# The attention half of a joint projection, placed in the second instead of the third input pass

## The chip, the cores and the metric

The kernel runs on one core of one Trainium2 chip. The metric is the device time of one execution, in microseconds; the time before is the median of three runs, 2733.04 us (2730.65 to 2734.66). The profile is of a further execution of the same program.

## The reference

One encoder layer on 2048 tokens of width 1024, in float32: a wide input projection, chunked band attention (8 heads) beside an mLSTM (4 heads), each projected back to the width and gated, an output projection, a squared-ReLU feed-forward layer and a last norm.

```python
xn = rms_norm(x, mix_norm_g)
aq, ak, av, mq, mk, mv, mo, ipre, fpre, ga, gm = jnp.split(xn @ w_in, points, axis=-1)
att = chunk_band_attention(heads(aq), heads(ak), heads(av), rel_bias)
mqk = jax.nn.silu(causal_depthwise_conv(jnp.concatenate([mq, mk], -1), conv_w, conv_b))
hm = mlstm_chunkwise(*heads(mqk), heads(mv), ipre + b_igate, fpre + b_fgate)
mlstm_out = jax.nn.sigmoid(mo) * head_rms_norm(hm, mh_norm_g)
y = jax.nn.sigmoid(ga) * (att @ w_att_proj) + jax.nn.sigmoid(gm) * (mlstm_out @ w_mlstm_proj)
x = x + y @ w_out
x = x + jnp.square(jax.nn.relu(rms_norm(x, ffn_norm_g) @ w_up)) @ w_down
return rms_norm(x, final_norm_g)
```

The two products in the line of `y` are what the change moves, for the first half of the tokens.

## The kernel before

**Blocks and products.** The tokens are four blocks of 512; blocks 0 and 1 make the first half, blocks 2 and 3 the second. Each float32 product is made of three matmuls of rounded parts (the operand is cast, and the remainder subtracted: one ScalarE and one VectorE instruction, called a split, lines 1348 and 1353 for activations, 582 and 584 for weights). The large products use a seven-product scheme: the operand matrix is cut in four quarters, from which sums are made (lines 1973 to 2015), seven products are formed, and their results are combined in `combine` (copies on ScalarE, line 2033, additions on VectorE, line 2041).

**The input projection of the second half** is written in three passes over its ten column groups, called names here, in the order `gm0, gm1, q, mq, vm, ga0, k, mk, ga1, mo` (`IN_ORDER`). Of the seven products, pass 1 makes those of `BATCHES[0]` (0, 3, 1), pass 2 those of `BATCHES[1]` (2, 4) and pass 3 those of `BATCHES[2]` (5, 6). A name takes 48 matmuls in pass 2 and in pass 3 (line 743), `vm` 96 (line 748). Between the passes, partial sums are parked in HBM (`park`), and up to six are loaded ahead. In passes 1 and 2 the names go one at a time; pass 3 takes them in pairs (`PAIRS`). The code numbers the passes g = 0, 1, 2, and a place in them (g, i).

**The operands of the passes** lie in `r` tiles, of which there are 28 in all (`rpool`). Sixteen of them form a ring for the passes: 12 for pass 1 and 4 of pass 2, and when pass 1 lets its 12 go, 4 more go to pass 2 and 8 to pass 3. Those eight are loaded from `xu` at the start of pass 2 (`take_batch`, `take_u1`, line 2346).

**The joint projection** of blocks 0 and 1 (`joint`) has two halves: half 0 is attention's product with `w_att_proj`, half 1 is the mLSTM's with `w_mlstm_proj`. Each half makes seven products for each of two column groups: 168 matmuls, at line 1134. Its operands are loaded from `mix`, where attention and mLSTM have stored their outputs (`take_joint`, line 1092): in two groups, one after the other, each with five `ctx` tiles (of 16) and four loads, and 14 `r` tiles in all. A half loads its 16 gate tiles through `temp` tiles (line 1167). Half 0 leaves its gated products in the four `sc` tiles and six `r` tiles, and half 1 adds to them (lines 1190 and 1205) and stores the sum `yp`, which the output projection loads.

Before the change, when pass 3 begins, the eight ring tiles that pass 2 has let go come back to `rpool`, the four `sc` and six `r` tiles are taken, and both halves' operands are asked for. Half 0 stands ahead of the third name of pass 3 (`q`), half 1 ahead of the fifth (`vm`). Ahead of `q`, eight more matmuls (line 1663) of the gate columns are made.

**What orders the work.** The kernel's steps are threads; a planner in the program steps them in a clock of its own, with a cost for each instruction, and writes each engine's instructions in the order in which they came. Where several are ready at once, the one goes first whose due time, computed back from a first pass of the planner, is the earliest. The order on each engine and on SP's DMA queue is then fixed; on the chip each instruction waits for its semaphores, and what is behind it waits with it. The dense products are one thread, in the order of the loops of `in_far`.

Of the kernel before, what the change touches and what calls it, by code (L numbers as in the profile page):

```python
# [52 lines left out]
BATCHES = ((0, 3, 1), (2, 4), (5, 6))  # L53
# [6 lines left out]
SUMS.update({at: N_Q - N_F + n for n, at in enumerate(((1, 1), (1, 6), *((4, i) for i in range(6))))})  # L60
SUMS.update({(0, 4): N_Q + 9, (0, 6): N_Q + 10})
J_ORDER = (0, 2, 3, 4, 5, 1, 6)
JOINT = {(2, 2): 0, (2, 4): 1}
PROJ = {2: (4, 0), 3: (6, 1)}

ORDER = (0, 1, 3, 2, 5, 4, 6)
# [241 lines left out]
def off(name):  # L308
    return 3 if name in ("mq", "mk") else 0
# [3 lines left out]
class Layer:  # L313
# [101 lines left out]
    def weights(self):  # L415
# [9 lines left out]
        for g, batch in enumerate(BATCHES):  # L425
            for pair in PAIRS if g == 2 else [(i,) for i in range(len(IN_ORDER))]:
                i = pair[0]
                if (g, i) in JOINT:
                    yield from (("half", (JOINT[g, i], t)) for t in range(7))
                vm = g == 0 and IN_ORDER[i] == "vm"  # L430
# [323 lines left out]
    def in_far(self, A, aev, ring):  # L754


        fl = self.fl
        E4 = lambda: [Event() for _ in range(NT)]
        pair = lambda of: [[of(), of()] for _ in IN_ORDER]
        kept = pair(E4)  # L760
        self.banks.want = 4
        for g, batch in enumerate(BATCHES):
            if g > 0:
                got, gev, room = ahead
            if g == 1:
                fl.spawn(self.take_batch(BATCHES[2], A, aev, ring), 1)
            if g == 2:
                fl.put(self.rpool, *(yield "get", ring, 8))
                J = [self.operands() for _ in range(2)]
                slots = (yield "get", self.sc, 4), (yield "get", self.rpool, 6), [[Event(), Event()] for _ in range(6)]  # L770
                fl.spawn(self.take_joint(0, J), 1)
            if g == 2:
                for pair in PAIRS:
                    if (g, pair[0]) in JOINT:
                        yield from self.joint(0, JOINT[g, pair[0]], J, slots)
                        if JOINT[g, pair[0]] == 1:
                            fl.put(room, *[0] * 4)
                    yield from self.in_last(pair, batch, A, aev, ring, got, gev, room)
                break
            for i, name in enumerate(IN_ORDER):  # L780
                self.sum_at(g + 1, i)
                if g < 2 and i == len(IN_ORDER) - 1:
                    ahead = pair(lambda: [None] * NT), pair(E4), Pool([0] * 6)
                    fl.spawn(self.unpark(g + 1, kept, *ahead), 1)
                if (g, i) in JOINT:
                    yield from self.joint(0, JOINT[g, i], J, slots)
                    if JOINT[g, i] == 1:
                        fl.put(room, *[0] * 4)
                tok = name == "vm"
                finish, o = (self.after_vm(), 0) if tok else (self.after_in(1, name), off(name))  # L790
                release = ring if i == len(IN_ORDER) - 1 else None
                bank, clear, every = [], E4(), range(NT if tok else 2)
                yield from self.product(tok, batch[0], A, aev, bank, None, release)
                if g == 0:
                    t, tev, other = [None] * NT, E4(), []
                    for n in every:
                        fl.spawn(self.park_first(n, t, tev[n], bank[n], clear[n], o), 1)
                    for m in batch[1:] if not tok else batch[:0:-1]:
                        if m == 3:
                            yield from self.product(tok, m, A, aev, other, None, release)  # L800
                            for n in every:
                                fl.spawn(self.park_u2(i, n, t, tev[n], other[n], kept[i][0][n], o), 1)
                        else:
                            yield from self.product(tok, m, A, aev, bank, clear, release)
                            for n in every:
                                fl.spawn(self.finish_ps(finish, n, bank[n]), 1)
                    if i == 1:
                        (bk,) = yield "get", self.banks, 1
                        yield from self.gate_mm(bk, A, ((0, 0), (1, 4)), True, True)
                        fl.spawn(self.gates(2, bk), 1)  # L810
                    continue
                for n in every:
                    fl.spawn(self.park_v(i, n, got[i], gev[i], bank[n], clear[n], kept[i][1][n], o) if g == 1 else
                             self.finish_far(finish, n, "a22", 1, got[i], gev[i], bank[n], clear[n], o, room), 1)
                yield from self.product(tok, batch[1], A, aev, bank, clear, release)
                for n in every:
                    fl.spawn(self.finish_far(finish, n, "a12" if g == 1 else "a21", 0, got[i], gev[i], bank[n], None,
                                             o, room), 1)
                if i == 1:
                    (bk,) = yield "get", self.banks, 1  # L820
                    yield from self.gate_mm(bk, A, ((2, 0),) if g == 1 else ((6, 8),), True, True)
                    fl.spawn(self.gates_kept(bk) if g == 1 else self.gates(3, bk, True), 1)
        self.banks.want = 0
        fl.put(self.rpool, *(yield "get", ring, 8))
# [241 lines left out]
    def project(self, b, room):  # L1066
# [14 lines left out]
        if b % 2 == 1:  # L1081
            O = self.y_operands = self.operands()
            for k in range(4):
                fl.spawn(self.take_y(b // 2, k, *O), 2)
    def take_joint(self, s, J):

        def row(x):
            def load(b, j, a):
                i = 4 * x + (j if j < 4 else j - 2)
                yield "wait", [self.blk[2 * s + b]["mix_ev"][i]]  # L1090
                yield "sp", 800, 2000
                self.nc.sync.dma_start(a, self.mixd.ap()[2 * s + b, i])

            return load

        for x in range(2):
            for k in range(2):
                yield from self.take_parts(row(x), 1.0, k, self.splitter(k, *J[x], 1.0), J[x][1], pool=self.ctx)

    def joint(self, s, x, J, slots):  # L1100

# [1714 lines left out]
```

## Time and profile before

| | |
|---|---|
| median of three runs | 2733.04 us |
| profiled execution | 2726.03 us |
| its span, first to last instruction | 2724.2 us |
| TensorE busy | 2706.6 us, 99% |
| VectorE busy | 2109.8 us, 77% |
| ScalarE busy | 1543.0 us, 57% |
| GpSimd busy | 48.4 us, 2% |
| mean granted clock of TensorE | 0.999 |
| moved by DMA | 683.01 MB, 251 GB/s |

Times in the profile are microseconds from the span's start. PE is TensorE's matmuls, PEld its weight loads, which run beside them; DVE is VectorE, ACT is ScalarE, POOL is GpSimd, and SPq is the queue in which SyncE issues DMAs. `L1134` is line 1134 of the kernel. A row of the timeline has the start, the length, the engine, the line, the operation with what it writes and reads, the count of instructions, and in brackets the idle time of the engine before it with what ended it. Matmuls overlap, so a row's length over its count is the time that one of them costs. In a row of DMA issues stand the count, the size of each and the median time from the issue to the landing.

The second pass's `ga0`, `k`, `mk`, `ga1`, `mo` are made from 832 to 887, the third pass from 887 to 1089; the output projection (line 712) follows.

### The profile page before, as it was taken

What the parts mean: (1) busy time and instruction counts of PE and PEld (TensorE: products, weight loads), DVE (VectorE), ACT (ScalarE), POOL (GpSimd) and SP (SyncE); (2) the same over time, 40 slices, a digit from 0 to 9 for tenths busy, and PEclk for the clock granted to TensorE, in tenths of its full rate; (3) what the DMA queues carried; (4) which work ended last, traced back from release to release, by engine and by line L of the source; (5) the groups of instructions that cost most, each with busy time, mean ns of one, the idle gap of its engine ahead of it and who ended that gap; (6) DMA issues with size and microseconds to landing.
All of it is one profiled execution on the core that took longest, in us unless ns stands there. A gap on an engine that the chain in (4) does not pass through costs nothing.

```text
span 2724.2 us, 38141 instructions
## 1 busy us (share of the span) xinstructions
PE 2706.6 (99%) x12784; PEld 2253.2 (83%) x12784; DVE 2109.8 (77%) x3750; ACT 1543.0 (57%) x2685; POOL 48.4 (2%) x79
## 2 busy tenths in 40 slices
PE   9999999999999999999999999999999999999998
PEld 8878888888888888888888888888888888888887
DVE  7878876888876899887768888889798665657675
ACT  6555456776753545566556766656345565554443
POOL 0000000000000000000000000000000000000000
PEclk9999999999999999999999999999999999999999
DMA  8777889878768889867768787766864454578863
GB/s 309 276 261 278 292 288 308 264 239 276 265 231 282 292 306 323 278 215 263 267 235 285 246 261 223 238 232 219 277 229 160 163 197 159 189 271 281 275 241 134
DMA packets 339304, 683.01 MB, mean 251 GB/s; under 512 B 37684, under 2 KB 66996, under 8 KB 339108
## 3 DMA queue, kind: packets, MB, share of 16 engines
q1 hardware_dynamic: 338388, 679.52, 73.2%
q8 instruction: 100, 1.64, 0.3%
q10 hardware_dynamic: 720, 1.06, 0.1%
q14 instruction: 96, 0.79, 0.1%
HBM read 461.41 MB, written 215.88 MB: 249 GB/s over the span
## 4 chain that ended last, share of the span: by engine, by line
PE 91%; DVE 3%; DMA 2%; issue 2%; ACT 1%; SPq 0%; POOL 0%; ACTq 0%; POOLq 0%; DVEq 0%
PE bank L712 40%; PE bank L743 9%; PE bank L644 8%; PE bank L645 8%; PE bank L643 8%; PE bank L1134 3%; PE bank L748 2%; PE bank L1612 2%; PE bank L1580 2%; PE bank L1505 2%; PE bank L970 1%; DVE wsp L584 1%; PE bank L1855 0%; PE bank L1840 0%; DMA ctx<-park 0%
## 5 line engine op out<-in xcount | busy, mean ns | idle before, releaser
L712 PE MATMUL bank<-r,wsp 128*128 128x512 f32 x4872 | 1110.3, 389 | 0.8 <-DVE wsp L584 0.7
L712 PEld LDWEIGHTS bank<-r,wsp 128*128 128x128 f32 x4872 | 913.2, 188 | 192.4 <-DVE wsp L584 1.2
L582 ACT CAST wsp<-wraw 128x1024 fp32r<-128x1024 f32 x437 | 459.1, 1051 | 495.3 <-PE bank L712 165.0
L584 DVE TENSOR_TENSOR wsp<-wraw,wsp 128x1024 fp32r<-128x1024 f32 x437 | 533.7, 1221 | 233.6 <-ACT wsp L582 228.6
L643 PE MATMUL bank<-r,wsp 128*128 128x512 f32 x960 | 379.3, 395 | 0.0
L645 PE MATMUL bank<-r,wsp 128*128 128x512 f32 x960 | 375.2, 391 | 0.0
L644 PE MATMUL bank<-r,wsp 128*128 128x512 f32 x960 | 375.2, 391 | 0.0
L743 PE MATMUL bank<-r,wsp 128*128 128x512 f32 x1512 | 368.1, 393 | 1.2 <-DVE ctx L894 1.0
L743 PEld LDWEIGHTS bank<-r,wsp 128*128 128x128 f32 x1512 | 279.0, 188 | 56.8 <-issue 1.0
L645 PEld LDWEIGHTS bank<-r,wsp 128*128 128x128 f32 x960 | 180.3, 188 | 38.4
L644 PEld LDWEIGHTS bank<-r,wsp 128*128 128x128 f32 x960 | 180.5, 188 | 33.6
L643 PEld LDWEIGHTS bank<-r,wsp 128*128 128x128 f32 x960 | 180.4, 188 | 33.4
L1353 DVE TENSOR_TENSOR r<-r 128x512 fp32r<-128x512 f32 x255 | 167.8, 683 | 19.1 <-ACT r L1348 18.3
L2041 DVE TENSOR_TENSOR ctx<-bank,ctx 128x512 f32<-128x512 f32 x174 | 118.9, 686 | 71.0 <-PE bank L712 69.7
L1348 ACT CAST r<-r 128x512 fp32r<-128x512 f32 x255 | 148.6, 616 | 32.0 <-DMA r<-u 28.6
L601 DVE TENSOR_TENSOR wraw<-wraw,wraw 128x1024 f32<-128x1024 f32 x112 | 136.3, 1218 | 3.3 <-DMA wsum<-wraw 2.3
L2033 ACT COPY ctx<-bank 128x512 f32<-128x512 f32 x174 | 101.1, 583 | 62.4 <-PE bank L712 46.5
L1593 ACT ACTIVATE sc<-sc,scs 128x640 f32<-128x640 f32 (+4 forms) x128 | 97.6, 763 | 68.6 <-DVE scs L1586 67.5
L2362 ACT ACTIVATE ctx<-ctx 128x512 f32<-128x512 f32 x96 | 60.5, 631 | 102.8 <-DVE ctx L2041 102.8
L1617 DVE TENSOR_TENSOR r<-bank,r 128x512 fp32r<-128x512 f32 (+1 forms) x168 | 95.7, 593 | 15.0 <-ACT r L1615 14.5
L1505 PE MATMUL bank<-r,r 128*128 128x512 f32 x336 | 94.8, 364 | 0.0
L1580 PE MATMUL bank<-r,r 128*128 128x256 f32 (+2 forms) x464 | 88.9, 312 | 1.6 <-DVE ctx L1896 0.7
(264 smaller groups left out, 3246.4 us busy)
## 6 DMA issues: line engine op xcount, KB each, us to landing
wraw<-in_wf SPq DMA_DIRECT2D x196, 512.0 KB, 4.8
r<-u SPq DMA_DIRECT2D x224, 256.0 KB, 4.1
wraw<-wsum SPq DMA_DIRECT2D x104, 512.0 KB, 4.9
u<-ctx SPq DMA_DIRECT2D x128, 256.0 KB, 2.2
ctx<-in_wf SPq DMA_DIRECT2D x104, 256.0 KB, 4.4
wsum<-ctx SPq DMA_DIRECT2D x104, 256.0 KB, 4.2
u<-tmp SPq DMA_DIRECT2D x96, 256.0 KB, 2.7
ctx<-park SPq DMA_DIRECT2D x66, 256.0 KB, 4.7
```

The lines of the kernel that those rows point to most:

```text
L582: nc.scalar.copy(w[:, 0], raw)
L584: nc.vector.tensor_sub(w[:, 1], raw, w[:, 0].bitcast(F32))
L601: V.tensor_sub(dst, x, y)
L643: mm(ps, lh, rh, start=first, stop=False)
L644: mm(ps, lh, rl, start=False, stop=False)
L645: mm(ps, ll, rh, start=False, stop=last)
L712: mm(ps, wv[:, x, k, n], a[:, y], start=new and k == 0 and x == y == 0, stop=k == 3 and x == 1, skip_group_check=True)
L743: mm(ps, wv[:, x, k, n], a[:, y], start=start and x == y == 0, stop=stop and x == 1, skip_group_check=True)
L1348: self.nc.scalar.copy(dst[:, 0], src)
L1353: self.nc.vector.tensor_sub(dst[:, 1], src, dst[:, 0].bitcast(F32))
L1505: nc.tensor.matmul(bkv[:, :, c0:c0 + w], st, sl[:, :, o:o + w], start=n == 0, stop=n == total - 1)
L1580: nc.tensor.matmul(bk[:, :c1 - c0], q[:, y, i * P:(i + 1) * P], kf[:, f * P + c0:f * P + c1], start=y == 0, stop=y == 1)
```

## The change

Half 0 moves from the third to the second pass, ahead of `mk` (place (1, 7)). Half 1 moves from the fifth name of pass 3 to the third, where half 0 was. The eight ring tiles that were loaded with pass 3's operands at the start of pass 2 stay empty until `ga0` (place (1, 5)); there they go to `rpool`, the `sc` and `r` tiles for the products are taken, and half 0's operands are asked for. When half 0 is done, eight `r` tiles go back to the ring, and pass 3's operands are loaded into them. Half 1's operands are asked for when pass 3 begins. Four more parked sums may be loaded ahead after half 1, as before, but that is now two names earlier. The order of the weights follows from `JOINT`.

```diff
 J_ORDER = (0, 2, 3, 4, 5, 1, 6)
-JOINT = {(2, 2): 0, (2, 4): 1}
+JOINT = {(1, 7): 0, (2, 2): 1}
+J_FROM = 5
...
         for g, batch in enumerate(BATCHES):
             if g > 0:
                 got, gev, room = ahead
-            if g == 1:
-                fl.spawn(self.take_batch(BATCHES[2], A, aev, ring), 1)
             if g == 2:
                 fl.put(self.rpool, *(yield "get", ring, 8))
-                J = [self.operands() for _ in range(2)]
-                slots = (yield "get", self.sc, 4), (yield "get", self.rpool, 6), [[Event(), Event()] for _ in range(6)]
-                fl.spawn(self.take_joint(0, J), 1)
+                fl.spawn(self.take_joint(0, 1, J), 1)
...
             for i, name in enumerate(IN_ORDER):
                 self.sum_at(g + 1, i)
+                if (g, i) == (1, J_FROM):
+                    fl.put(self.rpool, *(yield "get", ring, 8))
+                    J = [self.operands() for _ in range(2)]
+                    slots = (yield "get", self.sc, 4), (yield "get", self.rpool, 6), [[Event(), Event()] for _ in range(6)]
+                    fl.spawn(self.take_joint(0, 0, J), 1)
+                if (g, i) in JOINT:
+                    yield from self.joint(0, JOINT[g, i], J, slots)
+                    fl.put(ring, *(yield "get", self.rpool, 8))
+                    fl.spawn(self.take_batch(BATCHES[2], A, aev, ring), 1)
                 if g < 2 and i == len(IN_ORDER) - 1:
                     ahead = pair(lambda: [None] * NT), pair(E4), Pool([0] * 6)
                     fl.spawn(self.unpark(g + 1, kept, *ahead), 1)
-                if (g, i) in JOINT:
-                    yield from self.joint(0, JOINT[g, i], J, slots)
-                    if JOINT[g, i] == 1:
-                        fl.put(room, *[0] * 4)
...
-    def take_joint(self, s, J):
+    def take_joint(self, s, x, J):
...
-        for x in range(2):
-            for k in range(2):
-                yield from self.take_parts(row(x), 1.0, k, self.splitter(k, *J[x], 1.0), J[x][1], pool=self.ctx)
+        for k in range(2):
+            yield from self.take_parts(row(x), 1.0, k, self.splitter(k, *J[x], 1.0), J[x][1], pool=self.ctx)
```

## The prediction

> **What bounds the kernel now.** I read the head of the page first, then the table of windows, the timeline of TensorE, and last the DMA queue and VectorE.
>
> ```profile
> span 2724.2 us, 38141 instructions
> PE 2706.6 (99%) x12784; PEld 2253.2 (83%) x12784; DVE 2109.8 (77%) x3750; ACT 1543.0 (57%) x2685; POOL 48.4 (2%) x79
> ```
>
> TensorE is busy for all but 17.6 us of the span. No matmul is added or removed, so the change can only move idle time. The next rows are two windows: input pass 2 from `ga0` on (832.10 to 887.05), and input pass 3 (887.05 to 1088.90). Columns: length, busy us and count of PE, PEld, DVE, ACT, POOL, then clock, DMA share, GB/s.
>
> ```profile
> 832.10:887.05 54.95, 54.95 (x246) 45.52 (x245) 33.24 (x45) 18.29 (x23) 0.00 (x0) 1.00 0.84 285
> 887.05:1088.90 201.85, 199.62 (x877) 162.76 (x876) 185.27 (x281) 106.98 (x162) 0.00 (x0) 1.00 0.89 307
> ```
>
> VectorE is busy for 60% of the first stretch and for 92% of the second, at a higher DMA rate there. The timeline of TensorE (start, length, line, count, idle time before it):
>
> ```profile
> 832.08 2.89 PE L743 MATMUL bank<-r,wsp 128*128 128x512 f32 x12
> ...
> 908.71 2.01 PE L1663 MATMUL bank<-r,gw 128*40 128x512 f32 x8
> 910.57 2.24 PE L1134 MATMUL bank<-r,wsp 128*128 128x512 f32 x9
> ...
> 949.82 21.92 PE L743 MATMUL bank<-r,wsp 128*128 128x512 f32 x96
> 971.58 10.13 PE L1134 MATMUL bank<-r,wsp 128*128 128x512 f32 x44
> 982.97 28.44 PE L1134 MATMUL bank<-r,wsp 128*128 128x512 f32 x124 [1.26 <-ACT ctx L2033]
> 1011.25 21.92 PE L748 MATMUL bank<-wsp,r 128*128 128x512 f32 x96
> ...
> 1082.58 3.00 PE L743 MATMUL bank<-r,wsp 128*128 128x512 f32 x12 [0.45 <-DVE ctx L894]
> 1086.11 3.01 PE L743 MATMUL bank<-r,wsp 128*128 128x512 f32 x12 [0.53 <-DVE ctx L894]
> 1088.96 4.70 PE L712 MATMUL bank<-r,wsp 128*128 128x512 f32 x20
> 1094.40 15.98 PE L712 MATMUL bank<-r,wsp 128*128 128x512 f32 x69 [0.74 <-DVE wsp L584]
> ```
>
> From 949.82 to 971.58 there are 96 matmuls, 0.2267 us each. The 877 matmuls of pass 3 at that pitch take 198.8 us of its 201.85, so only 3.1 us can be won there, and 0.74 behind it. The two halves of the joint projection (line 1134, 168 matmuls, 38.1 us each) stand at 910.57 and 971.58. The first one waited for its operands, as the view of that line says among what ended the idle time before it:
>
> ```profile
>   DVE r L1353: 0.3, 1
> ```
>
> **The change, part by part.** I call the end of `vm` in pass 2 T (832.08). After the change the attention half starts two names later, T + 2 x 48 x 0.2267 = T + 21.8, and its operands are asked for at T. In the old place they were asked for at T' = 887.05 and needed at 910.57, T' + 23.5: two names and the eight gate matmuls of 908.71, which have no counterpart in the new place. So the lead is 1.7 us shorter. The whole half lasts 38.1 us in either place.
>
> Are the inputs there? The attention of the first two blocks must be done. The view of the tile `sc` between 700 and 1000 (first and last start) shows its last transposes:
>
> ```profile
> L1612 PE MATMUL bank<-const,sc x52: 270/272/274, 701.2 to 756.6; 128*128 128x128 f32 x52
> ```
>
> That is 75 us ahead of T, so the four `sc` tiles and attention's `r` tiles are free. The last mLSTM head still runs. These are rows of the DMA queue around T:
>
> ```profile
> 829.78 3.54 SPq L2286 DMA_DIRECT2D mvfar<-ctx  x4
> ...
> 836.33 0.32 SPq L1541 DMA_DIRECT2D mix<-ctx  x1
> ```
>
> That head holds one `r` tile and four of the 16 `ctx` tiles until its last store at 836.33, T + 4.25. At T four more `ctx` are being stored for `vm` and six hold parked sums, which leaves two. The loads of the operands need five at once, so I take them to start at T + 4.25. In the old place nothing held `ctx` in this way; the `r` tiles came late instead. Its rows, DMA queue, ScalarE and VectorE:
>
> ```profile
> 872.52 0.45 SPq L1092 DMA_DIRECT2D ctx<-mix  x1
> ...
> 885.06 0.43 SPq L1092 DMA_DIRECT2D ctx<-mix  x1
> ...
> 903.25 0.38 SPq L1092 DMA_DIRECT2D ctx<-mix  x1
> ```
>
> ```profile
> 893.64 0.62 ACT L1348 CAST r<-ctx 128x512 fp32r<-128x512 f32 x1
> ```
>
> ```profile
> 909.52 0.68 DVE L2008 TENSOR_TENSOR ctx<-ctx,ctx 128x512 f32<-128x512 f32 x1
> 910.12 1.22 DVE L584 TENSOR_TENSOR wsp<-wraw,wsp 128x1024 fp32r<-128x1024 f32 x1
> 911.26 0.68 DVE L1353 TENSOR_TENSOR r<-ctx,r 128x512 fp32r<-128x512 f32 x1
> ```
>
> The first split stood at 893.64, T' + 6.6, since the tiles came free at T'; the first split of the second group at 911.26, just when it was needed. In the new place the first load can land at T + 4.25 + 4.2 (the median below), so the first split stands at T + 8.45, 1.85 us later against its start than in the old place. **The new wait** ahead of the attention half is therefore 0.3 + 1.7 + 1.85 = 3.9 us. Its bounds: 0, if a VectorE at 60% and tiles that are free at once make good for it, and 0.3 + 1.7 + 4.25 = 6.25, if the whole wait for `ctx` is passed on. I take 3.9, the value that follows from the row of the first split.
>
> Transfers of the stretch (counts from 700 to 1100, size, median to landing):
>
> ```profile
> tmp<-gate SPq DMA_DIRECT2D x32, 256.0 KB, 3.9
> ...
> ctx<-mix SPq DMA_DIRECT2D x16, 256.0 KB, 4.2
> wraw<-wsum SPq DMA_DIRECT2D x16, 256.0 KB, 4.7
> ...
> r<-xu SPq DMA_DIRECT2D x12, 256.0 KB, 4.4
> wraw<-in_wf SPq DMA_DIRECT2D x12, 256.0 KB, 5.1
> r<-tmp SPq DMA_DIRECT2D x12, 256.0 KB, 5.1
> ```
>
> One half issues 8 loads of mixer outputs, 16 of gates, 14 of half weights and 12 stores of partial products: 50 issues on SP, some 20 us of its time by 0.4 us each, moved past the stores and loads of `mk`, `ga1`, `mo`. POOL has no work in the part that moves. On VectorE the half brings 14 splits, 8 sums, 12 additions and 16 products at 0.68 and 7 weight subtractions at 1.22: 42.5 us. The eight operand tiles of the last pair of products, loaded some 80 us earlier now, come behind it: 8 loads, 8 x 0.62 on ACT, 8 x 0.68 = 5.4 on DVE. From T to the start of pass 3 there are then 54.95 + 38.1 = 93.1 us with 33.24 + 42.5 + 5.4 = 81.1 us of VectorE (87%), and pass 3 keeps 142.8 of 163.8 us (87%). Both fit, so I cost the moved work itself at nothing.
>
> The third pass's operands I cost at nothing too: the work that hides them is `mk`, `ga1`, `mo`, 3 x 10.9 = 32.7 us, against 4.4 to land and the first four splits (5.2 us of both engines). They are DMAs into tiles that TensorE has just read, so SP waits there for TensorE, and the weights of `ga1` stand behind it; the oldest eight of the 14 tiles are read 8 us before the half ends, which covers that. Without the cover, pass 3 starts 4.4 + 1.3 late.
>
> The mLSTM half now has the place, the lead and the neighbours that the attention half had: 0.3 us, which before stood there too. The 1.26 at 982.97 was ScalarE waiting for a `ctx` tile behind the convolutions of `mq`; they now come after the half, so it goes: -1.3 (bounds -1.3 and 0). The 0.45 and 0.53 at the end of pass 3 are VectorE late at 92%; at 87% I take half away, -0.5 (bounds -1 and +1). The 0.74 behind them falls in the rush for the output projection's last operands, whose tiles still come free with the last products: 0 (bounds -0.7 and +1). What the new order of pass 2 does to attention and mLSTM before T: 0, bounded by 1.3 either way, the largest idle of this stage.
>
> Sum: 3.9 - 1.3 - 0.5 = +2.1 us on the profiled 2726.0, that is 2728.1. The median of the three runs shown is 2733.0, 7.0 above the profiled execution, and the same +2.1 gives 2735.1, +0.08%.
>
> **The rivals.**
>
> No wait, all idle gone: the operands come in time and 1.26 + 0.98 + 0.74 + 0.3 = 3.3 us go: 2729.7. For it speaks that VectorE is at 60% there. To be faster by over 0.2% (5.5 us, about what a measurement of this kernel can tell from no change), idle time of other stages has to go as well; the waits shown between 832 and 1110 don't hold so much.
>
> Slower, by one mechanism: the operands are taken in two groups of five `ctx` tiles, and each group waits for them. The second group then pays again about one landing, 4.2, on top of 6.25, less the 1.8 won: +8.7, 2741.7. It decides from the point where the first split of the second group stands later than T + 30 (needed at T + 22.5, and 5.5 + 1.8 more). For it: the old place has that split just in time and the new one has less lead. Against: the second group follows the first in its own tiles.
>
> Transfers become the bound: the stretch moved 285 GB/s x 54.95 = 15.7 MB, and 50 + 8 transfers of 0.262 MB add 15.2: 30.9 MB in 93.1 us, 332 GB/s. At the 307 of pass 3 it takes 100.7 us, +7.6 less 1.8 is +5.8: 2738.8. Against it stands a window of pass 3, the `vm` name, that went at 356 without idle time on TensorE:
>
> ```profile
> 1011.20:1033.00 21.80, 21.80 (x97) 18.04 (x97) 19.49 (x30) 8.22 (x11) 0.00 (x0) 1.00 0.99 356
> ```
>
> The Trainium skill, "DMA: Bandwidth & Descriptors" (Specifications), puts the limit of HBM for one core at about 358 GB/s; the trace agrees, its densest stretch stands at 356 with a share of 0.99. By that rule 332 passes on average, with little room for bursts, and the sum stays.
>
> The clock falls after the wait: if TensorE ran the first product of the half, 12 matmuls, at half its rate, that adds 2.7: 2737.8. The granted clock is 1.00 in each window quoted, and no idle piece above is longer than 1.26 us. The Trainium skill, "TensorE: Matmul & The Clock Gate" (HAM oscillation), says that an idle gap of over some 3.4 us brings the clock down to half; no run here shows such a gap, and the wait that I forecast would be the first that is long enough.
>
> That the change doesn't do what it says (the half is placed, but waits for attention) is excluded by the 75 us above.
>
> **How the numbers follow.** A wait of two to six us with a part of the idle time gone has 0.42, no wait at all 0.20, the double wait 0.22, transfers as the bound 0.10, the fallen clock 0.06. The double wait, the transfers and the upper end of the first case (0.06) are slower by over 0.2%: 0.38. Half of the second case and the least of the first are faster: 0.12. The rest, 0.50, is within. The likeliest case alone reaches from 2731 to 2738. The range goes from 2727 (no wait, all idle gone, and something besides) to 2745 (the double wait with one more landing, less a part that other waits hide); about 1 in 10 is left out on either side.
>
> **What would show it.** In the changed profile line 1134 stands first near 854, then near 950. Right: idle time of about 4 us ahead of its first matmuls, ended by the split (line 1353), and none for `ctx` in the second half; the loads of mixer outputs begin near T + 4; VectorE near 87% in both stretches; pass 3's first product starts without a wait. Wrong: no idle time at the first half (then it is 2730 or less), or idle time ahead of the first products of pass 3, or a loss in a stage that I left at nothing, such as the output projection.

## The result, and the profile after

The changed kernel takes 2735.77 us in the median of 14 runs (2731.62 to 2742.13), the kernel before 2731.97 in 14 runs beside them. The ratio is 1.0019, with a 95% interval of 1.0012 to 1.0026: 3 to 7 us slower, by about 5. The forecast for that median was 2735.1, a step of 2.1.

Head of the page of the changed kernel:

```profile
span 2737.1 us, 38133 instructions
PE 2710.2 (99%) x12784; PEld 2254.2 (82%) x12784; DVE 2108.9 (77%) x3752; ACT 1540.6 (56%) x2683; POOL 50.1 (2%) x79
```

Its span is 12.9 us longer than that of before, more than the medians differ, so I first cut it in stages by fixed instructions: the first matmul of pass 1, T (the end of `vm` in pass 2, as in the prediction), and M, the first matmul of the row sums behind the output projection (line 2306 before, 2307 after).

```
            start to pass 1   pass 1 to T   T to M   M to end
before           453.6            378.5      611.8     1280.3
after            458.0            377.2      619.2     1282.7
```

Of the 12.9 us, 4.4 lie ahead of pass 1. There the instructions of both kernels stand in the same order on every engine (the first difference comes in pass 1, near 690 us), so this part is not the change; the last section comes back to it. T to M holds everything that the change moves: +7.4. It is one execution of each kernel. Nine of the profiles below have the same instructions in the same order up to 817 us, and their pass 1 to T takes 377.2 to 381.9 us, so a difference of two or three us between two stages of single executions, as the -1.3 and +2.4 of the table, means little by itself. Idle time of TensorE in T to M was 611.80 - 608.83 = 3.0 before and is 619.20 - 610.49 = 8.7 after; the other 1.7 of the 7.4 lie in the matmuls' own time. The windows of T to M of the two kernels (before, then after; columns as in the prediction):

```profile
832.10:1443.90 611.80, 608.83 (x2681) 500.88 (x2680) 497.34 (x690) 328.25 (x482) 0.11 (x1) 1.00 0.79 273
```

```profile
835.20:1454.40 619.20, 610.49 (x2682) 500.31 (x2681) 500.82 (x698) 332.29 (x490) 0.11 (x1) 1.00 0.79 271
```

Where it idles, the timeline of TensorE of the changed kernel shows:

```profile
857.46 38.66 PE L1135 MATMUL bank<-r,wsp 128*128 128x512 f32 x168
...
958.76 35.23 PE L1135 MATMUL bank<-r,wsp 128*128 128x512 f32 x153 [1.66 <-ACT r L1349]
993.82 21.92 PE L744 MATMUL bank<-r,wsp 128*128 128x512 f32 x96
...
1027.53 11.14 PE L749 MATMUL bank<-wsp,r 128*128 128x512 f32 x48 [0.91 <-DVE ctx L896]
...
1081.40 8.02 PE L744 MATMUL bank<-r,wsp 128*128 128x512 f32 x34 [1.32 <-DVE ctx L896]
1089.26 5.15 PE L713 MATMUL bank<-r,wsp 128*128 128x512 f32 x22
1097.43 5.73 PE L744 MATMUL bank<-r,wsp 128*128 128x512 f32 x24 [3.03 <-DVE ctx L896]
...
1106.95 13.40 PE L713 MATMUL bank<-r,wsp 128*128 128x512 f32 x56 [0.84 <-ACT r L1351]
```

The attention half (857.46) runs without a break. The loss stands in the mLSTM half, behind its first 15 matmuls (1.66), and in the names behind it (0.91 + 1.32 + 3.03), where TensorE waits for a bank that VectorE's addition of a parked sum (line 896) must free. Why VectorE is late shows in its own timeline and in that of the queue:

```profile
1072.69 0.69 DVE L896 TENSOR_TENSOR ctx<-bank,ctx 128x512 f32<-128x512 f32 x1 [0.64 <-DMA ctx<-park]
...
1090.56 0.69 DVE L896 TENSOR_TENSOR ctx<-bank,ctx 128x512 f32<-128x512 f32 x1 [0.86 <-DMA ctx<-park]
```

```profile
1087.14 0.63 SPq L2287 DMA_DIRECT2D kfar<-tmp  x1
1091.95 0.32 SPq L2287 DMA_DIRECT2D gate<-ctx  x1
1092.31 1.40 SPq L885 DMA_DIRECT2D ctx<-park  x3
```

From 1087.77 to 1091.95 the queue issues nothing: it stands at the store of a gate tile that ScalarE writes only at 1091.29. Three loads of parked sums stand behind that store and are issued from 1092.31 on, when the product that they are added to is already next on TensorE. From 1090.56 until TensorE goes on at 1097.43, VectorE itself has no idle time. The question for the experiments: is it tiles, the order of the queue, or the rate of the transfers that makes the sums late, or is VectorE simply full?

First the rate. From the end of the mLSTM half to the last product of pass 3, before and after:

```profile
1011.25:1089.00 77.75, 76.78 (x338) 62.96 (x337) 71.04 (x113) 42.16 (x65) 0.00 (x0) 1.00 0.92 325
```

```profile
993.82:1097.43 103.61, 98.36 (x431) 80.29 (x430) 96.88 (x152) 53.02 (x80) 0.00 (x0) 1.00 0.94 322
```

Before, 325 GB/s x 77.75 us = 25.3 MB passed beside 338 matmuls, 76.6 us at 0.2267: without idle time that asks for 330 GB/s. After, it is 33.4 MB beside 431 matmuls, 97.7 us: 341. This alone doesn't name the rate: wherever TensorE idles, for whatever cause, the rate reached is below the one asked for. Nor is 325 a ceiling. Within that stretch of the kernel before, 12 us run at 403 GB/s and 4 us at 103:

```profile
1047.25:1059.25 12.00, 12.00 (x54) 9.94 (x54) 9.75 (x17) 8.42 (x14) 0.00 (x0) 1.00 1.05 403
1067.00:1071.00 4.00, 4.00 (x19) 3.32 (x18) 3.72 (x9) 2.98 (x5) 0.00 (x0) 1.00 0.27 103
```

And the loads of parked sums don't land later after their issue than before, where the landing was seen (the two stretches, before, then after):

```profile
ctx<-park SPq DMA_DIRECT2D x19, 256.0 KB, 6.1
```

```profile
ctx<-park SPq DMA_DIRECT2D x28, 256.0 KB, 5.1
```

The same two windows hold the other candidate. VectorE's work was 71.04 us beside 76.6 us of matmuls, and is 96.88 beside 97.7: it had 5.6 us to spare and now has 0.8. What it loses in waiting, for parked sums 2.50 us in all and for casts of weights 1.93, it can hardly make up.

In the kernel before, the two halves stood among the names of pass 3 with a lower rate: attention half, two names, mLSTM half:

```profile
910.57:948.70 38.13, 38.13 (x169) 30.61 (x168) 35.35 (x54) 20.63 (x33) 0.00 (x0) 1.00 0.82 273
949.80:971.58 21.78, 21.78 (x97) 18.02 (x96) 21.40 (x35) 12.38 (x18) 0.00 (x0) 1.00 0.95 328
971.58:1011.40 39.82, 38.56 (x170) 31.60 (x169) 38.20 (x57) 17.13 (x26) 0.00 (x0) 1.00 0.84 289
```

After the change only one such pause is left in pass 3, and two names earlier.

### The profile page after: what moved, and what is told of

It is laid out like the page before. It is cut to its first block, busy times and chain, and to the rows that moved or that the text cites. A ratio compares the mean times of both kernels' runs of the same rounds, so it can differ in the third digit from the quotient of the medians.

```text
span 2737.1 us, 38133 instructions
## 1 busy us (share of the span) xinstructions
PE 2710.2 (99%) x12784; PEld 2254.2 (82%) x12784; DVE 2108.9 (77%) x3752; ACT 1540.6 (56%) x2683; POOL 50.1 (2%) x79
## 4 chain that ended last, share of the span: by engine, by line
PE 82%; DVE 8%; DMA 5%; ACT 2%; issue 2%; SPq 0%; POOL 0%; ACTq 0%; DVEq 0%; POOLq 0%
PE bank L713 34%; PE bank L644 8%; PE bank L645 8%; PE bank L646 8%; PE bank L744 8%; PE bank L749 2%; PE bank L1613 2%; PE bank L1581 2%; PE bank L1506 2%; DVE wsp L585 2%; PE bank L972 1%; PE bank L1135 1%; DMA x<-ctx 1%; DMA wraw<-in_wf 1%; DVE r L1354 1%
## 5 line engine op out<-in xcount | busy, mean ns | idle before, releaser
L646 PEld LDWEIGHTS bank<-r,wsp 128*128 128x128 f32 x960 | 180.2, 188 | 38.5
L645 PEld LDWEIGHTS bank<-r,wsp 128*128 128x128 f32 x960 | 180.5, 188 | 33.4
L644 PEld LDWEIGHTS bank<-r,wsp 128*128 128x128 f32 x960 | 180.4, 188 | 33.4
```

Source lines behind the costliest of these rows:

```text
L644: mm(ps, lh, rh, start=first, stop=False)
L645: mm(ps, lh, rl, start=False, stop=False)
L646: mm(ps, ll, rh, start=False, stop=last)
```

## The experiments

All ratios are to the kernel before, timed on the same chip in the same rounds. T to M is from one profiled execution each, and the waits listed are those that bear on the argument.

**Room for four parked sums given back at its old place.** The change also gives the room for four more parked sums back at another place, behind the half at (2, 2). Here it comes ahead of `vm`, as before.

```
+                    if pair[0] == 4:
+                        fl.put(room, *[0] * 4)
...
-                        if JOINT[g, pair[0]] == 1:
-                            fl.put(room, *[0] * 4)
```

> Only the four additional parked sums go back to their old place, ahead of vm; both halves of the projection stay where the change put them. Theory A (the third group of the output projection's operands takes its five ctx tiles some 20 us earlier and keeps them until pass 3 lets its r tiles go, so parked sums come late): no change within 1 us, still about 5 us slower than the kernel before, and TensorE still waits some 4 us for additions at the end of pass 3. Theory B (the four additional parked tiles, two names earlier, are what fills the ctx tiles): the waits at the end of pass 3 go, and the time comes to within 2 us of the kernel before. Theory C (only the late operands of the mLSTM half, 1.7 us, are the change's doing, and the rest is the luck of one execution): no change.

Ratio 1.0035 [1.0023, 1.0047], T to M 618.1. The end of pass 3 now held a wait of 0.83 us and one of 4.60, at a product of the output projection. The place of that room alone is not the cause. The wait in the mLSTM half was 0.70 here; in this run and in two others below (1.14 and 1.25) the order of the queue up to that wait is the changed kernel's, so its 1.66 is the largest of four executions.

**The mLSTM half in its old place.** The parked sums' room and the output projection's operands, which hang on that half, go back with it.

```
-JOINT = {(1, 7): 0, (2, 2): 1}
+JOINT = {(1, 7): 0, (2, 4): 1}
```

> The attention half stays in pass 2, the mLSTM half goes back to its old place ahead of vm, and with it the output projection's operands and the four parked sums. Theory A: the waits at the end of pass 3 go, and so does the 1.7 us ahead of the mLSTM half, whose operands then have 46 us; within 2 us of the kernel before, or faster than it by up to 3 us. Theory B: the same. Theory C: the 1.7 us go, 3 us slower than before remains or less.

Ratio 1.0010 [1.0001, 1.0019], T to M 614.1. No wait in the mLSTM half, and 0.24 + 0.16 at the end of pass 3 and behind it, but a new one within `vm`:

```profile
1023.97 12.79 PE L749 MATMUL bank<-wsp,r 128*128 128x512 f32 x48 [3.41 <-DVE ctx L896]
```

By the ratios about half of the loss belongs to the mLSTM half's earlier place and what hangs on it, though the two intervals overlap. With the attention half alone moved, the kernel is still not faster than before.

**Output projection's operands asked for later.** They are loaded from the end of the mLSTM half on; here from `vm` on.

```
+                    if pair[0] == 4:
+                        O = self.y_operands = self.operands()
+                        for k in range(4):
+                            fl.spawn(self.take_y_late(0, k, O), 2)
...
-        if x == 1:
-            O = self.y_operands = self.operands()
-            for k in range(4):
-                fl.spawn(self.take_y_late(s, k, O), 2)
```

> Both halves stay where the change put them; only the loads of the output projection's operands are started at their old place, ahead of vm, instead of right after the mLSTM half. Theory A: the waits for additions at the end of pass 3 (4.4 us in the profile of the change) go, the 1.7 us ahead of the mLSTM half stay: 1 to 2.5 us slower than the kernel before. Theory B: the four parked tiles are still early, so about 5 us slower as the change is. Theory C: no change.

Ratio 1.0032 [1.0020, 1.0045], T to M 623.2. The end of pass 3 still held 1.55 + 0.27, `vm` 2.42, and the output projection, whose operands were now late, 0.67, 1.68 and 0.94 us ended by their splits. Asking later for them moves the loss and takes none of it away.

**The attention half's operands asked for one name later.**

```
-J_FROM = 5
+J_FROM = 6
```

> The attention half's operands are asked for at k instead of ga0, 10.9 us later, and everything else as in the change. The prediction's step held that ctx tiles free at T + 4.25 set the first load; the profile of the change shows the first load at T - 15 and the last at T + 18 and no wait. If the lead of 21.8 us was just enough, TensorE now waits 7 to 11 us at the first matmuls of line 1135, and the time rises by that. If the lead had room to spare (the DMA queue runs ahead of TensorE), the wait is under 4 us.

Ratio 1.0044 [1.0031, 1.0058], T to M 625.8. Now the half does wait for its operands, inside and not ahead of its first matmuls, where I had forecast the wait:

```profile
857.16 4.24 PE L1135 MATMUL bank<-r,wsp 128*128 128x512 f32 x18
863.26 2.34 PE L1135 MATMUL bank<-r,wsp 128*128 128x512 f32 x9 [1.87 <-DVE wsp L585]
868.82 33.94 PE L1135 MATMUL bank<-r,wsp 128*128 128x512 f32 x141 [3.21 <-ACT ctx L2034]
```

```profile
867.66 0.62 ACT L1349 CAST r<-ctx 128x512 fp32r<-128x512 f32 x1 [6.91 <-DMA ctx<-mix]
```

The copy that ended the 3.21 stands on ScalarE behind that cast, which had waited 6.91 us for a load of operands. The half lasts 45.4 us instead of 38.5. So a lead of 10.9 us costs about 7, and one of 21.8 nothing.

From 966 us to M this run has the changed kernel's instructions in the same order on every engine and on SP, and it has the same waits for additions, 1.25 + 1.33 + 2.88 = 5.46 us against 0.91 + 1.32 + 3.03 = 5.26:

```profile
1087.84 8.02 PE L744 MATMUL bank<-r,wsp 128*128 128x512 f32 x34 [1.33 <-DVE ctx L896]
1095.70 5.15 PE L713 MATMUL bank<-r,wsp 128*128 128x512 f32 x22
1103.72 7.36 PE L744 MATMUL bank<-r,wsp 128*128 128x512 f32 x24 [2.88 <-DVE ctx L896]
```

So the loss behind the mLSTM half is not the chance of one execution. It belongs to what is written.

**Two more `ctx` tiles**, in the changed kernel and, as a control, in the kernel before. The two bias tiles lie unused from the end of attention to the row sums; they are lent to the pool.

```
                     yield from self.in_last(pair, batch, A, aev, ring, got, gev, room)
+                self.recall()
...
+                if (g, i) == (1, 5):
+                    fl.spawn(self.lend(), 1)
...
+    def lend(self):
+        pool, home = self.ctx, self.bias
+        pool.lent = yield "get", home, 2
+        pool.home, pool.recalled = home, False
+        self.fl.put(pool, *pool.lent)
```

> The changed kernel with two more ctx tiles: the two bias tiles, which attention has left by then, are lent to that pool from ga0 of pass 2 to the end of pass 3. Three theories of the 5 to 7 us that the changed kernel loses from ga0 of pass 2 to the mid of the output projection (its T to M is 619.2 us, before 611.8). Tiles: the parked sums come late because the 16 ctx tiles are taken; then the 1.66 ahead of the mLSTM half and most of 1.32 + 3.03 at the end of pass 3 go, T to M is below 614 and the ratio to the kernel before is 0.9990 to 1.0005. Queue: the parked loads stand behind stores on SP that wait; tiles change nothing, ratio 1.0015 to 1.003, T to M 618 to 620. Rate: the stretch behind the mLSTM half already moves 320 to 325 GB/s at a DMA share of 0.92 to 0.98, so the loads land late wherever they are issued; tiles change nothing either, and the loads are issued earlier but land as late.

> The kernel before with the same two lent tiles, as the control. Tiles: its 1.26 ahead of the mLSTM half's second quarter and its 0.45 + 0.53 at the end of pass 3 can go, -1 to -2.5 us, ratio 0.9990 to 0.9996. Queue and rate: no change, ratio 0.9997 to 1.0003.

After with them: 1.0024 [1.0015, 1.0033], T to M 617.6, with 2.60 us ended by line 915 (the addition of parked sums there) still at the end of pass 3. Before with them: 1.0013 [1.0004, 1.0021], T to M 615.7. Two more tiles help neither kernel, so tiles alone are not what is short. In the changed kernel waits of 0.72 and 1.30 came up elsewhere, at the attention half and behind it.

**Loads of parked sums ahead of all else on SP.**

```
-                yield "sp", 800, 2000
+                yield "sp!" if g == 2 else "sp", 800, 2000
                 self.nc.sync.dma_start(t[:, o:o + 512], self.parkd.ap()[i, x, n])
```

> The changed kernel with the loads of parked sums for pass 3 put ahead of all else that SP could issue at the time. Queue: the additions no longer wait for parked sums, 3 to 5 us come back, ratio 0.9997 to 1.0008, T to M 613 to 616. Tiles: a load can't be issued before its tile is free, so the waits stay, ratio 1.0015 to 1.003. Rate: what lands earlier here lands later elsewhere (weights or convolution inputs), ratio 1.0015 to 1.003 with idle time ended by weights.

Ratio 1.0006 [0.9997, 1.0015], T to M 615.2: half of the 7.4 us of T to M is gone, and by the ratio two thirds of the loss, as the queue theory had it. What is left: 1.50 in the mLSTM half, 0.60, 0.87, and 1.22 at the output projection. Behind the mLSTM half it moved 325 GB/s, hardly more than the 322 above. That made the queue the leading theory, to be tested where it should do the same.

**The same urgency elsewhere:** with urgent loads of the mLSTM half's operands too (the word "sp!" in `take_joint` for x = 1), in the kernel before, and with the mLSTM half in its old place.

> The changed kernel with urgent loads of parked sums for pass 3 (ratio 1.0006 alone, T to M 615.2 us) and now urgent loads of mixer outputs for the mLSTM half too. Queue: the 1.50 that is left ahead of the mLSTM half is the last of eight loads that SP issues behind gate stores and weights; it goes, T to M 613.5 to 614.5, ratio 0.9999 to 1.0004. Rate or tiles: the wait stays or moves into the name behind the half, T to M 615 to 617, ratio 1.0004 to 1.0012.

> The kernel before with the same urgent loads of parked sums, as the control. If the order of SP's queue is a loss that the change alone made, nothing moves here: ratio 0.9997 to 1.0003, T to M 611 to 612.5. If the same loss stands in the kernel before (its 0.45 + 0.53 at the end of pass 3), up to 1 us goes: 0.9994 to 0.9997. Then the changed kernel with urgent loads is still 1 to 3 us behind its own control.

> The attention half in pass 2 as in the changed kernel, the mLSTM half in its old place, loads of parked sums urgent. The run without urgency had T to M 614.1 and one wait of 3.41 us within vm, behind the mLSTM half, where VectorE's additions stood behind products that waited for gates (1.37, 1.89, 2.17 us), and the granted clock at 0.72 in the 6 us behind it. If that wait is a matter of parked loads it goes, T to M 609 to 611, ratio 0.9990 to 0.9998, the only version that would beat the kernel before. If it is the gates, as the releaser says, it stays: T to M 613 to 615, ratio 1.0003 to 1.0012.

None of the three came out as the order of the queue alone would have it: 1.0019 [1.0007, 1.0031], 1.0024 [1.0015, 1.0033] and 1.0020 [1.0011, 1.0030], with T to M 618.1, 618.3 and 616.3. With the mLSTM half's loads urgent the wait in that half grew to 2.10, and one of 2.14 for weights came in `vm`. With the mLSTM half in its old place the 3.41 in `vm` did go, so it was not the gates alone, but 0.47, 1.78 and 0.80 came in the output projection. In the kernel before, urgent parked sums made the weights and operands of the output projection late:

```profile
1103.36 7.56 PE L712 MATMUL bank<-r,wsp 128*128 128x512 f32 x32 [2.22 <-ACT wsp L582]
1112.45 8.05 PE L712 MATMUL bank<-r,wsp 128*128 128x512 f32 x32 [1.53 <-ACT r L1350]
```

In each of these runs what is put first lands in time, and something else lands late. That speaks for a shortage that a new order only hands on; what is short, the transfers' rate or VectorE's time, these runs don't tell.

**Half of the output operands later.** The third and fourth group of the output projection's operands are asked for ahead of `mo`.

```
+                    if pair[0] == 9:
+                        for k in range(2, 4):
+                            fl.spawn(self.take_y_late(0, k, self.y_operands), 2)
...
-            for k in range(4):
+            for k in range(2):
                 fl.spawn(self.take_y_late(s, k, O), 2)
```

> The changed kernel with the third and fourth group of the output projection's operands (16 loads, 4.2 MB with their far tiles) asked for only ahead of mo, the first two as before. Rate: 4.2 MB less of some 19 MB in the last 59 us of pass 3, so the waits of 1.32 and 3.03 there shrink to under 1, and idle time inside the output projection takes their place if its operands are late (the run with all four groups late had 0.67 + 1.68 + 0.94 there): ratio 1.0005 to 1.002. Tiles: the five ctx tiles of the third group are free from 1052 to 1087, so the same gain at the end of pass 3, and the tiles theory can't be told from rate by this run alone. Queue: little change, ratio 1.0015 to 1.003.

Ratio 1.0010 [1.0001, 1.0018], T to M 617.5. One wait of 2.16 at the end of pass 3, where I had expected under 1, and 1.72 + 0.56 + 0.34 in the output projection: a trade of the kind that the rate theory expects, though this run can't tell it from the tiles theory.

**Half of the stores' columns.** This run alone takes bytes away. The stores that pass 3 makes for the last block pass `cut=True`, and the other half of those tensors is set to zero near the start; the kernel leaves out that half of the last block's values.

```
-    def store(self, dst, src, ev, pool=None, item=None, queue="sp"):
+    def store(self, dst, src, ev, pool=None, item=None, queue="sp", cut=False):
         yield queue, 800, 2000
+        if cut:
+            dst, src = dst[:, :256], src[:, :256]
         self.nc.sync.dma_start(dst, src)
...
```

> The changed kernel, but the stores that pass 3 makes for the last block (gates, far q and k, convolutions, mLSTM values: 48 tiles) write only half of their columns; the other half of these tensors is set to zero once near the start. This part of the last block is left out, so the output isn't the reference's. The order of the instructions on every engine stays nearly the same (under 3% moved, most of it ahead of pass 1), no load gets smaller, and every ctx tile is held as long as before by its producers. In the stretch from the end of the mLSTM half to the last product of pass 3 about 36 of these stores, 4.7 MB of the 33.5 MB, go away: 28.8 MB in 97.7 us of matmuls asks for 295 GB/s in place of 343. Rate: the additions no longer wait for parked sums, the 1.32 and 3.03 us shrink to under 0.5 each and the 1.66 ahead of the mLSTM half shrinks too; T to M 611 to 615 us against 619.2, ratio 0.9990 to 1.0005 (the early zeros may cost 1 or 2 us ahead of pass 1). Queue: the loads are issued behind the same stores in the same order, so the waits stay within 1 us of what they were; T to M 618 to 620, ratio 1.0015 to 1.003.

T to M is 610.9: 8.3 less than in the changed kernel, and 0.9 less than before. Of the idle time, 0.59 in the mLSTM half and 1.85 at the last product are left, none in between:

```profile
967.65 0.73 PE L1142 MATMUL bank<-r,wsp 128*128 128x512 f32 x2 [0.59 <-DVE r L1361]
...
1005.07 21.92 PE L751 MATMUL bank<-r,wsp 128*128 128x512 f32 x96
1026.83 22.26 PE L756 MATMUL bank<-wsp,r 128*128 128x512 f32 x96
1048.93 49.12 PE L751 MATMUL bank<-r,wsp 128*128 128x512 f32 x216
...
1104.66 5.75 PE L751 MATMUL bank<-r,wsp 128*128 128x512 f32 x24 [1.85 <-DVE ctx L903]
```

Its window from the end of the mLSTM half to that last product:

```profile
1005.07:1104.66 99.59, 97.69 (x431) 80.25 (x429) 96.38 (x152) 52.62 (x80) 0.00 (x0) 1.00 0.91 301
```

30.0 MB in place of 33.4 ask for 307 GB/s beside the same matmuls. VectorE has the same work, 96.38 us, and waits for parked sums only 0.71 us. The 1.85 that is left is VectorE's own: it goes from one instruction to the next there without idle time. In total this kernel took 1.0047 [1.0029, 1.0064], where I had expected at most 1.0005: the zeros that it writes near the start put pass 1 at 470.1 in place of 458.0, 12 us where I had put 1 or 2. Its time as a whole therefore says nothing, only its stages do.

I had expected the order of the instructions to stay as it was. On SP's queue it did not. Of the changed kernel's 139 issues from 958 to 1098 us about one in six stands elsewhere, and among them is the store that the last parked sums stood behind: here they go ahead of it, and the queue doesn't stand.

```profile
1094.24 0.46 SPq L2296 DMA_DIRECT2D kfar<-tmp  x1
1094.75 2.39 SPq L892 DMA_DIRECT2D ctx<-park  x4
...
1099.17 0.32 SPq L2296 DMA_DIRECT2D gate<-ctx  x1
```

So this run changes the bytes and the order at once, and can't be put down to the bytes. A shorter store also lands sooner (those to `mfar` in 3.0 us in the median against 4.1), and so do the parked sums, in 4.4 against 5.1.

**What stands.** Most of the loss lies in the names behind the mLSTM half and comes back with the written order. There the transfers (341 GB/s asked for; over the 71 to 105 us behind that half the runs with all their bytes reached 313 to 338) and VectorE (0.8 us to spare) are both near their end, and the longest wait follows four us in which the queue stood at a store. Moving one kind of load ahead gained once and lost in its neighbours, and no version was faster than the kernel before; the best, urgent parked sums in the changed kernel, can't be told from it. Which of the three, rate, VectorE's time or the order of the queue, makes the loss stays open. A run with the bytes cut in the very order of the changed kernel, or with work taken from VectorE there, would tell; neither was made.

## Why the prediction was right or wrong, point by point

The number was right by luck, and the main term of its sum was not. The forecast was +2.1; the ratio gives +3.3 to +7.1, and T to M of the two profiles +7.4. A wait of 3.9 us that didn't come was made up for by 4.3 and 1.7 us in places that I had put at a gain and at nothing, and the forecast's base, the median of the first three runs, lay 1.1 us above that of all fourteen. In idle time of TensorE the terms below add up to -1.3 + 1.7 + 4.3 + 0.85, and 0.2 between the two halves, 5.7 of the 7.4. My own sign of being wrong, no idle time at the attention half, came as well, but not with the 2730 or less that I had tied to it.

- **The new wait ahead of the attention half, +3.9 (0 to 6.25): 0.** I let the first load start when the last mLSTM head gives its tiles back, T + 4.25. The first loads stand at 819.76, 15.4 us ahead of T = 835.20:

```profile
819.76 0.32 SPq L1094 DMA_DIRECT2D ctx<-mix  x1
```

  Its first split was then at 842.07, T + 6.9, where I had T + 8.45, so the instant was near. But I priced the wait by moving the old place's 0.3 with the first split, and misread that 0.3. It was idle time of the weight loads (PEld), 9.8 us into the half, and ended with the last split of the second group; the matmuls lost nothing there:

```profile
919.61 0.68 DVE L1353 TENSOR_TENSOR r<-ctx,r 128x512 fp32r<-128x512 f32 x1
```

  So neither its size nor its start was the thing to shift. A second mistake lies under it: "asked for at T" is a place in the written order, and the queue passes that place as soon as its waits allow. The first load that I showed for the old place, 872.52, was already 14.5 us ahead of T'. The run with a later request has the wait and shows that, by an estimate from its 10.9 us less lead and the 5.1 us that it waited, some 6 us of the lead are to spare.
- **1.26 in the mLSTM half gone: -1.3, as forecast.** No wait for `ctx` stands in that half after. Whether it went for my reason, that the convolutions of `mq` now come later, is not shown: with the half back in its old place, behind `mq`, it was gone too.
- **The mLSTM half's own wait, 0: +1.66.** I argued that it inherits the place and lead of the attention half. Its last load of operands was issued at 950.77, among gate stores and weights:

```profile
950.77 0.43 SPq L1094 DMA_DIRECT2D ctx<-mix  x1
...
957.08 0.62 ACT L1349 CAST r<-ctx 128x512 fp32r<-128x512 f32 x1 [3.02 <-DMA ctx<-mix]
```

  Urgency did not mend it. With half the stores it was 0.59, but 0.70 also came with the changed kernel's own bytes and order.
- **The end of pass 3, -0.5 (-1 to +1): +4.3** (0.91 + 1.32 + 3.03 against 0.45 + 0.53). This is the term that failed with its sign and its bounds. I took VectorE's share of the whole pass, 92%, and its fall as a gain at the end. VectorE did fall in pass 3 as a whole, to 149.38 of 168.70 us, 89%, but in the names behind the mLSTM half its work rose from 93% to 99% of the matmuls' time (71.04 of 76.6 us, 96.88 of 97.7), and the transfers asked for rose from 330 to 341 GB/s. An average over the pass hid the stretch.
- **Pass 3's operands, 0: 0.** Pass 3 starts without a wait. **The output projection, 0 (-0.7 to +1 at its start): +0.85** (0.84 there, and 0.75 at 1171.20, against 0.74).
- **The moved work in pass 2, at nothing: right.** T to the start of pass 3 took 93.50 us, where I had 93.1, with 75.29 us of VectorE where I had 81.1.

```profile
835.20:928.70 93.50, 93.30 (x411) 76.30 (x410) 75.29 (x110) 42.92 (x63) 0.00 (x0) 1.00 0.89 300
```

- **The rivals.** "Transfers become the bound" had a price (+5.8) near what came, at the wrong place; whether it had the right mechanism is open, as said above. I looked for it where work was added. There it ran at 300 GB/s, not 332, without a wait. The loss came where work was taken away: the halves, at 273 and 289 GB/s in their old windows, had been stretches of fewer transfers between names that ask for more, and the stretch without one grew from 78 to 104 us. The Trainium skill, "DMA: Bandwidth & Descriptors" (Specifications), has a limit of about 358 GB/s for one core, as half of what two cores share. I said that the trace agreed, by a window of 22 us at 356. It does not: 12 us of the same kernel run at 403 (above), so the measurement decides, and 358 was no bound to reason from here. The double wait of the attention half did not come; a wait for its second group came when the operands were asked for later. The fallen clock came there too, and at other places (below).

T to M agrees with the timed ratios over all versions, roughly, which is why I read the places of the loss from it: 614.1 to 617.5 go with 1.0006 to 1.0020, 617.6 to 619.2 with 1.0019 to 1.0035, 623.2 and 625.8 with 1.0032 and 1.0044 (leaving out the run with fewer bytes).

## What to carry to other kernels

Where a piece of work is moved out of a stretch, ask not only whether the new place has room, but what the old place loses: here a piece with fewer transfers had stood between names with more, and the GB/s of the windows with and without it show that. For each stretch that is left, not for the pass as a whole, divide the work of each engine, and the bytes, by the time of its matmuls. Where two of them come near the end at once, as here VectorE at 99% and 341 GB/s, look for idle time there before looking at the new place.

When urgent loads help in one kernel and hurt in its neighbour, expect of a new order only that it chooses who waits. And when a run takes something away to find a cause, compare the order of the queue in its trace with that of the kernel it stands for: here the program that writes the order moved about one issue in six, and the run could no longer tell bytes from order.

## What the runs showed of the hardware that I had not expected

**The clock falls after idle times well below 3.4 us, and not after each.** In the run with later output operands, after 0.67 and 1.68 us of idle time within 5 us (windows; the last three columns are clock, DMA share, GB/s):

```profile
1105.90:1110.15 4.25, 2.56 (x10) 1.80 (x11) 3.58 (x7) 1.96 (x5) 0.00 (x0) 1.00 0.93 318
1110.15:1112.00 1.85, 1.85 (x5) 1.23 (x6) 1.31 (x2) 0.58 (x1) 0.00 (x0) 0.70 0.90 274
1112.00:1114.00 2.00, 2.00 (x6) 1.55 (x5) 1.70 (x3) 1.05 (x1) 0.00 (x0) 0.50 0.91 313
1114.00:1116.00 2.00, 2.00 (x10) 1.65 (x9) 2.00 (x4) 1.18 (x2) 0.00 (x0) 0.92 0.27 101
```

In the changed kernel itself, after a longer wait, of 3.03 us, it stays at full speed:

```profile
1094.50:1097.40 2.90, 0.00 (x0) 0.00 (x0) 2.90 (x5) 1.13 (x2) 0.00 (x0) 1.00 0.96 343
1097.40:1100.00 2.60, 2.57 (x11) 2.15 (x12) 2.31 (x3) 2.27 (x4) 0.00 (x0) 1.00 0.98 300
```

At the same place of the run with the later request, whose instructions are the same there, it fell after 2.88 us:

```profile
1103.70:1107.00 3.30, 3.28 (x10) 2.62 (x11) 2.30 (x3) 2.90 (x4) 0.00 (x0) 0.69 0.90 297
```

It also fell after 2.14 us (the run with both kinds of load urgent), and after 3.41 (0.72 over the next 6 us, the run with the mLSTM half in its old place) and 4.60 (0.50 over 4 us, the run with the room at its old place); it did not after 2.10, 2.16 and 2.22 in others. A fall costs about 2 us beside the wait (38 matmuls in 10.90 us behind the 1.68, where 0.2267 each gives 8.6). The Trainium skill, "TensorE: Matmul & The Clock Gate" (HAM oscillation), names gaps of over some 3.4 us; here shorter ones were enough in some cases, so the measurement decides.

**Two executions of the same instructions differ by up to 6 us ahead of pass 1.** In the profiles, leaving out the run with half of the stores' columns, pass 1 starts between 453.6 and 459.9. The changed kernel's, at 458.0, shows a reason:

```profile
221.35 25.04 PE L713 MATMUL bank<-r,wsp 128*128 128x512 f32 x102 [2.59 <-DVE ctx L2042]
```

```profile
221.35:224.00 2.65, 2.65 (x7) 2.10 (x8) 2.65 (x6) 2.34 (x5) 0.00 (x0) 0.61 0.31 116
```

A wait of 2.59 us for an addition, and behind it 102 matmuls in 25.04 us, where 0.2267 each gives 23.1: 2.6 + 1.9 = 4.5, about the whole difference of 4.4 to the kernel before. The profile of before has no such wait between 200 and 300 us. What makes it come in one execution and not in the next was not tried.
